# A trunk of attention and HGRN2 heads on one core: a head's output is multiplied and copied out of PSUM before its norm scale is known

## The chip, the core and the metric

One core of a Trainium2 chip runs the whole kernel. TensorE (PE) multiplies matrices and writes only to PSUM; VectorE (DVE) and ScalarE (ACT) read PSUM and SBUF; GpSimd (POOL) works on SBUF; SyncE (SP) issues most of the transfers. Each engine works through its own queue in order, and semaphores tie the queues together. The metric is the time of one execution on the device in microseconds, as a median of runs.

## What is computed

Two layers run over 256 latent tokens and 256 context tokens of 1024 channels. Each layer mixes tokens with three parallel branches (differential attention, a gated MLP over chunks, a bidirectional HGRN2), merges them, and ends with a convolutional FFN. Layer 0 computes context outputs too (512 tokens), layer 1 only the latent ones (256). What the change touches is the end of the first and the third branch, where each head's output is normed over its 128 channels:

```python
def att_out(o):
    return (rmsnorm(o, att_subln_g) * (1 - lam_init)).reshape(o.shape[0], o.shape[1], ATT_VW)

def hg_out(o, g):
    Bo, To = o.shape[0], o.shape[1]
    o = rmsnorm(o.astype(h.dtype), hg_norm_g) * jax.nn.silu(g.reshape(Bo, To, HG_HEADS, HG_DV))
    return o.reshape(Bo, To, HG_VW)
```

## The kernel before

Each of the two layers goes through a stage of heads, a gMLP stage, a merge of the branches, an output product and an FFN. Weights come from HBM as 128x1024 tiles on SP's queue (L110), are cast to a rounded high part on ScalarE (L111) and a low part on VectorE (L112), and every large product is three matmuls into one PSUM bank (L121 to L123).

In the stage of heads the loop runs over eight heads. While the large products of head h+1 are made ("main": gates L371 to L375, softplus and silu L354 to L363, rotary embedding L577 to L585, values L405), two generators work off head h: `hg_head` and `att_head`. `weave` interleaves them: main is cut into steps, and each generator's `yield`s are spread over them. So TensorE's order is written out by the program (its schedule is set to manual), while ScalarE, VectorE and GpSimd get theirs from a planner, which takes what is ready and, of that, what the program traced first. Nothing in this order changes at run time.

There are two pools of four PSUM banks: "pm" for the large products, "ps" for all else. A head's output `o` is a "ps" tile of 128 channels by NQ tokens (512 in layer 0, 256 in layer 1), which lies in one bank until its last reader is done. For the norm, `rms_square` squares it on ScalarE (L316) and splits the square in a high part (ScalarE, L192) and a low part (VectorE, L193, tile "sqs"). In a later step `rms_scale` sums both over the channels with a product by all ones on TensorE (L321), and takes Ln (L327) and Exp (L328) on ScalarE; the result r is the reciprocal root, in tile "sq".

Then r is multiplied with the output: in `hg_head` by L550, which reads `o`, the norm weight "hgn" and r, and by L551, which multiplies with the gate `gg` (half of the tile "qg"); in `att_head` by L644, which reads `o`, the factor `av[:, 1:2]` and r. The result is stored to HBM on SP's queue (L943) and read again in the merge. So `o` holds its bank over the ones product, Ln, Exp, and L550 or L644.

Around this place VectorE also works off the levels of the next HGRN head: differences L441 (followed by an Exp, L442, on ScalarE), products L445, and the masked copies L465 from a "ps" bank; and attention's scores (L602 on TensorE, maxima L605 on VectorE, Exp L608 on ScalarE), turned weights (L619, L621, tile "wt" with two buffers), and value products (L626). GpSimd multiplies in L447, L460, L579 and L585.

Of the kernel before, what the change touches and what calls it, by code (L numbers as in the profile page):

```python
# [13 lines left out]
AF = mybir.ActivationFunctionType  # L14
# [3 lines left out]
P = 128  # L18
# [29 lines left out]
def trunk(ctx: ExitStack, tc: tile.TileContext, A, out):  # L48
    nc = tc.nc
    sub, mul, add, amin, amax = ALU.subtract, ALU.mult, ALU.add, ALU.min, ALU.max  # L50
# [9 lines left out]
    @contextmanager  # L60
    def pool(name, side="left", **tags):
        with tc.tile_pool(name=name, bufs=1, side=side, reuse_waits="tile") as p:
            def get(tag, shape, dt=F32):
                return p.tile(shape, dt, tag=tag, name=tag, bufs=tags[tag])
            yield get
# [10 lines left out]
    def PS(shape):  # L76
        return psm.tile(shape, F32, tag="ps", name="ps")
# [22 lines left out]
    def pk(l, n):  # L100
        a, b = PK[n]
        return pack[l][:, a:b]
# [88 lines left out]
    def split(t, src):  # L191
        nc.scalar.copy(out=t[:, 0, :], in_=src)  # L192
        nc.vector.tensor_tensor(out=t[:, 1, :], in0=src, in1=t[:, 0, :].bitcast(F32), op=sub)  # L193
        return t
# [119 lines left out]
    def rms_square(get, o, n):  # L314
        sq = get("sq", [P, 512])
        nc.scalar.activation(out=sq[:, :n], in_=o, func=AF.Square)  # L316
        return sq, split(get("sqs", [P, 2, n], F32R), sq[:, :n])
# [5 lines left out]
    def rms_scale(sq, n):  # L323
        sq, parts = sq
        ms = PS([P, 512])
        column_sums(ms[:, :n], parts)
        nc.scalar.activation(out=sq[:, :n], in_=ms[:, :n], func=AF.Ln, scale=1.0 / P, bias=epsb)  # L327
        nc.scalar.activation(out=sq[:, :n], in_=sq[:, :n], func=AF.Exp, scale=-0.5)  # L328
        return sq
# [78 lines left out]
    def hg_head(get, l, h, z, k, q, gg, v, put, lbv, C0, NQ):  # L408
# [3 lines left out]
        if l > 0:  # L412
            s = get("E", [P, 2, NT])
            nc.scalar.activation(out=s, in_=z, func=AF.Exp)
            for d in range(2):
                nc.vector.tensor_scalar(out=s[:, d, :], in0=s[:, d, :], scalar1=lbv[:, 1, d, h:h + 1], scalar2=2.0 ** -60,
                                        op0=mul, op1=amax)
                nc.scalar.activation(out=s[:, d, :], in_=s[:, d, :], func=AF.Ln, bias=lbv[:, 0, d, h:h + 1])
                nc.vector.scalar_tensor_tensor(out=z[:, d, :], in0=z[:, d, :], scalar=lbv[:, 2, d, h:h + 1], in1=s[:, d, :],
                                               op0=add, op1=amin)  # L420
# [118 lines left out]
        o = PS([P, NQ])  # L539
        for s in range(NS):  # L540
# [3 lines left out]
            if s == 0:  # L544
                for d in range(2):
                    nc.tensor.matmul(o[:, c], lhsT=st[:, d, :], rhs=V[:, d, 0:T], start=False, stop=(d == 1))  # L546
        sq = rms_square(get, o, NQ)
        yield
        r = rms_scale(sq, NQ)
        nc.vector.scalar_tensor_tensor(out=r[:, :NQ], in0=o, scalar=pk(l, "hgn"), in1=r[:, :NQ], op0=mul, op1=mul)  # L550
        nc.vector.tensor_tensor(out=r[:, :NQ], in0=r[:, :NQ], in1=gg, op=mul)  # L551
        put(r[:, :NQ])

# [34 lines left out]
    def att_head(get, l, qk, v, put, av, NQ):  # L588
        sc = 64 ** -0.5
        o = None  # L590
# [39 lines left out]
        for i in range(n + 2):  # L630
# [3 lines left out]
            if 2 <= i:  # L634
                if o is None:
                    o = PS([P, NQ])
                values(i - 2, *ws.pop(i - 2))
            if 1 <= i <= n:
                ws[i - 1] = turn(*ps.pop(i - 1))
                yield  # L640
        sq = rms_square(get, o, NQ)
        yield
        r = rms_scale(sq, NQ)
        nc.vector.scalar_tensor_tensor(out=r[:, :NQ], in0=o, scalar=av[:, 1:2], in1=r[:, :NQ], op0=mul, op1=mul)  # L644
        put(r[:, :NQ])
        yield

# [193 lines left out]
    with pool("x0", side="right", x=4, n=4, h=4, wa=5, wb=5, scr=1, cr=1, wj=1) as get, \  # L841
# [19 lines left out]
        av = cp.tile([P, 2, 8], F32, tag="av00", name="av")  # L861
# [31 lines left out]
        for t0 in (0, 2):  # L893
            r = []
# [41 lines left out]
    for l in range(DEPTH):  # L936
        ns = 4 if l == 0 else 2
        NQ = ns * P
# [28 lines left out]
        with pool("heads", lk=2, qg=1, qk=1, v=3, w=2, sq=2, sqs=2 if l else 1, wt=2, sc=1, E=6 if l else 4, K=2, p=2) as get, ExitStack() as even, \  # L967
# [22 lines left out]
            for h in range(HEADS):  # L990
                j = slice((h % 2) * P, (h % 2 + 1) * P)
                m = [hg_head(get, l, h, d["ls"], d["k"], d["qg"][:, 0, :], d["qg"][:, 1, :], d["vh"][:, :, j], putter(1, h),
                             lbv, (reset, masks), NQ),
                     att_head(get, l, d["qk"], d["va"][:, :, j], putter(0, h), attv[l], NQ)]
                if h + 1 < HEADS:
                    main, n = project(h + 1, d), units(h + 1)
                else:
                    even.close()
                    getv = rvt.enter_context(pool("vt", side="right", vt=ns))
                    vt = [getv("vt", [P, D]) for _ in range(ns)]  # L1000
                    pus = []
                    main, n = tail_proj(l, Xh, vt, ns, NQ, pus), 8 * ns // 2 + ns
                weave(main, n, m, (13, 2 * ns + 3), 0.92 if h + 1 < HEADS else (0.7, 0.85)[l])
# [4 lines left out]
        with pool("off", off=1) as off, pool("yT", yT=4) as get, ExitStack() as ygpool:  # L1008
            off("off", [P, (64, 48)[l]])
            yT = [get("yT", [P, 2, NQ]) for _ in range(4)]  # L1010
            get = ygpool.enter_context(pool("yg", ws=2, yg=4))
# [200 lines left out]
```

## Time and profile before

| | us |
|---|---|
| median of 3 runs | 2232.55 |
| lowest, highest | 2230.82, 2233.64 |
| profiled execution, its own time | 2240.42 |
| its span, first to last instruction | 2238.6 |
| mean granted TensorE clock in it | 0.981 of full speed |

The profile is that of one execution. Busy times are per engine; the share of a stretch is what matters, since the stages have different limits. The two stages of heads lie at about 100 to 640 us (layer 0) and 1440 to 1850 us (layer 1). A group's mean mixes shapes unless the view keeps them apart, and a wait is put down to the instruction that came last.

### The profile page before, as it was taken

To read this page: it belongs to the slowest core of one execution; us is meant where nothing else is said; L and a number is where in the kernel's file an instruction comes from. 1 tells how busy PE (TensorE), PEld (TensorE's weight loads), DVE (VectorE), ACT (ScalarE), POOL (GpSimd) and SP (SyncE) were. 2 spreads that over 40 slices of the span, in tenths; PEclk is the share of its full clock that TensorE was granted. 3 is DMA by queue.
4 is the path that set the end of the run, shared out by engine and by line. 5 is a ranking of instruction groups with operands and counts; after the bars stand their busy time and mean duration, and the time that the engine had idled before them with its cause. 6 is when DMAs were issued, how large, how long until landed. Compare 5 with 4: busy or idle time off the path is not lost. (4 is left out here: it accounts for less than half of the span.)

```text
span 2238.6 us, 32836 instructions
## 1 busy us (share of the span) xinstructions
PE 2136.9 (95%) x12448; PEld 1860.9 (83%) x12448; DVE 1713.4 (77%) x2869; ACT 1155.8 (52%) x1920; POOL 315.7 (14%) x272
## 2 busy tenths in 40 slices
PE   8999999999999998989999998999999989997998
PEld 7888788887888886878887877988888879997997
DVE  6799888989767884358776766898899976567786
ACT  3766665656543223245342334666666655455664
POOL 3332132322200000011000002222221210001000
PEclk9999999999999999999999999999999999998999
DMA  7212212212255754344555653322222336654554
GB/s 283 94 67 73 70 66 76 73 65 66 62 174 193 235 161 112 94 159 136 166 187 182 198 148 105 104 91 90 81 90 86 97 99 218 195 183 142 186 194 138
DMA packets 93488, 293.21 MB, mean 131 GB/s; under 512 B 16017, under 2 KB 20753, under 8 KB 93073
## 3 DMA queue, kind: packets, MB, share of 16 engines
q1 hardware_dynamic: 93042, 290.59, 40.1%
q8 instruction: 98, 1.61, 0.3%
q14 instruction: 60, 0.49, 0.1%
q10 hardware_dynamic: 288, 0.52, 0.1%
HBM read 282.66 MB, written 8.41 MB: 130 GB/s over the span
## 5 line engine op out<-in xcount | busy, mean ns | idle before, releaser
L121 PE MATMUL pm<-X,wh 128*128 128x512 f32 (+1 forms) x2032 | 716.1, 352 | 11.0 <-DVE X L255 6.5
L122 PE MATMUL pm<-X,wh 128*128 128x512 f32 (+1 forms) x2032 | 699.0, 344 | 0.0
L123 PE MATMUL pm<-X,wl 128*128 128x512 f32 (+1 forms) x2032 | 698.8, 344 | 0.0
L112 DVE TENSOR_TENSOR wl<-wr,wh 128x1024 fp32r<-128x1024 f32 (+1 forms) x402 | 496.8, 1242 | 203.5 <-ACT wh L111 198.9
L111 ACT CAST wh<-wr 128x1024 fp32r<-128x1024 f32 x408 | 422.0, 1039 | 310.7 <-PE pm L122 172.2
L121 PEld LDWEIGHTS pm<-X,wh 128*128 128x128 f32 x2032 | 386.8, 190 | 61.2 <-DVE X L255 7.9
L123 PEld LDWEIGHTS pm<-X,wl 128*128 128x128 f32 x2032 | 387.1, 190 | 47.3
L122 PEld LDWEIGHTS pm<-X,wh 128*128 128x128 f32 x2032 | 386.5, 190 | 42.1
L225 DVE SCALAR_TENSOR_TENSOR wj<-wa,scr 128x1024 f32<-128x1024 f32 x128 | 156.4, 1222 | 63.4 <-DMA wa<-in_ada_row 60.4
L447 POOL TENSOR_TENSOR K<-qg,E 128x512 f32<-128x512 f32 (+1 forms) x96 | 132.3, 1380 | 461.9 <-PE ps L507 304.3
L121 PE MATMUL pm<-wl,X 128*128 128x256 f32 (+1 forms) x608 | 188.0, 309 | 0.0
L122 PE MATMUL pm<-wh,X 128*128 128x256 f32 (+1 forms) x608 | 183.7, 302 | 0.0
L123 PE MATMUL pm<-wh,X 128*128 128x256 f32 (+1 forms) x608 | 183.7, 302 | 0.0
L202 POOL TENSOR_TENSOR s<-s,mhalf 128x1 f32<-128x1 f32 x26 | 14.3, 550 | 1078.4 <-DVE s L199 1052.7
L121 PE MATMUL pm<-ys,wh 128*128 128x512 f32 (+1 forms) x384 | 129.9, 338 | 10.6 <-ACT wh L111 7.4
L441 DVE TENSOR_TENSOR E<-lk 128x512 f32<-128x512 f32 (+1 forms) x192 | 124.4, 681 | 9.5 <-PE ps L546 8.1
L123 PE MATMUL pm<-ys,wl 128*128 128x512 f32 (+1 forms) x384 | 129.5, 337 | 0.0
L122 PE MATMUL pm<-ys,wh 128*128 128x512 f32 (+1 forms) x384 | 129.5, 337 | 0.0
L121 PEld LDWEIGHTS pm<-wl,X 128*128 128x128 f32 x608 | 117.7, 194 | 6.5 <-issue 2.2
L122 PEld LDWEIGHTS pm<-wh,X 128*128 128x128 f32 x608 | 117.8, 194 | 4.0
L123 PEld LDWEIGHTS pm<-wh,X 128*128 128x128 f32 x608 | 117.4, 193 | 4.2
L442 ACT ACTIVATE E<-E 128x1024 f32<-128x1024 f32 (+1 forms) x96 | 80.9, 846 | 59.9 <-DVE E L441 58.9
(250 smaller groups left out, 3541.3 us busy)
## 6 DMA issues: line engine op xcount, KB each, us to landing
wr<-in_w_up SPq DMA_DIRECT2D x88, 512.0 KB, 4.4
wa<-in_ada_row SPq DMA_DIRECT2D x80, 512.0 KB, 4.1
wr<-in_w_gate SPq DMA_DIRECT2D x48, 512.0 KB, 4.0
wr<-in_w_dn SPq DMA_DIRECT2D x40, 512.0 KB, 4.1
wr<-in_w_hqg SPq DMA_DIRECT2D x32, 512.0 KB, 3.6
wr<-in_w_hff SPq DMA_DIRECT2D x32, 512.0 KB, 3.6
wr<-in_w_aqk SPq DMA_DIRECT2D x32, 512.0 KB, 3.6
wr<-in_w_hi SPq DMA_DIRECT2D x16, 512.0 KB, 4.0
```

The source lines that it names most:

```text
L111: nc.scalar.copy(out=hi, in_=raw)
L112: eng.tensor_tensor(out=lo, in0=raw, in1=hi.bitcast(F32), op=sub)
L121: nc.tensor.matmul(ps, lhsT=lh, rhs=rl, start=first, stop=False)
L122: nc.tensor.matmul(ps, lhsT=lh, rhs=rh, start=False, stop=False)
L123: nc.tensor.matmul(ps, lhsT=ll, rhs=rh, start=False, stop=last)
L202: nc.gpsimd.tensor_tensor(out=r, in0=r, in1=mhalf, op=ALU.pow)
L225: nc.vector.scalar_tensor_tensor(out=junk, in0=raw, scalar=1.0, in1=scr[:, v, :], op0=mul, op1=mul, accum_out=mod[l][:, m, v:v + 1])
L441: nc.vector.tensor_tensor(out=dst, in0=ref if first else src, in1=src if first else ref, op=sub)
L442: nc.scalar.activation(out=E, in_=E, func=AF.Exp)
L447: nc.gpsimd.tensor_tensor(out=mkap(KQ[:], dims, NQ), in0=mkap(q, dims), in1=mkap(E[:], [[2 * b, np_], [b - NQ, 2], [1, b]], NQ), op=mul)
```

## The change

Both normalisations read `o` ahead of the `yield` that follows the square, and no more behind it.

In `hg_head` the product of `o` with the norm weight and the gate is made first, in place of the gate's tile, on VectorE; behind the Exp one product with r is left. The number of VectorE instructions and their sizes stay.

In `att_head` ScalarE copies `o` times the factor to a tile `u`, taken from the tag "wt" of the turned weights; behind the Exp VectorE multiplies r with `u`, both in SBUF, in place of the product that read `o` from PSUM. Each head has one ScalarE instruction more, 16 in all.

```diff
@@ hg_head
         sq = rms_square(get, o, NQ)
+        nc.vector.scalar_tensor_tensor(out=gg, in0=o, scalar=pk(l, "hgn"), in1=gg, op0=mul, op1=mul)
         yield
         r = rms_scale(sq, NQ)
-        nc.vector.scalar_tensor_tensor(out=r[:, :NQ], in0=o, scalar=pk(l, "hgn"), in1=r[:, :NQ], op0=mul, op1=mul)
         nc.vector.tensor_tensor(out=r[:, :NQ], in0=r[:, :NQ], in1=gg, op=mul)
         put(r[:, :NQ])
@@ att_head
         sq = rms_square(get, o, NQ)
+        u = get("wt", [P, NQ])
+        nc.scalar.activation(out=u, in_=o, func=AF.Copy, scale=av[:, 1:2])
         yield
         r = rms_scale(sq, NQ)
-        nc.vector.scalar_tensor_tensor(out=r[:, :NQ], in0=o, scalar=av[:, 1:2], in1=r[:, :NQ], op0=mul, op1=mul)
+        nc.vector.tensor_tensor(out=r[:, :NQ], in0=r[:, :NQ], in1=u, op=mul)
         put(r[:, :NQ])
         yield
```

## Rows read from the trace of the kernel before

**Rows 1.** The page's first part: busy us of an engine, share of span, instructions.

```profile
PE 2136.9 (95%) x12448; PEld 1860.9 (83%) x12448; DVE 1713.4 (77%) x2869; ACT 1155.8 (52%) x1920; POOL 315.7 (14%) x272
```

**Rows 2.** Stretches of heads: stretch, length, busy us by engine, granted clock, DMA.

```profile
core 0: us, PE busy (x) PEld busy (x) DVE busy (x) ACT busy (x) POOL busy (x), PEclk, DMA share, GB/s
100.00:640.00 540.00, 521.65 (x3010) 443.95 (x3009) 453.92 (x781) 323.32 (x566) 144.61 (x89) 0.99 0.21 71
1440.00:1850.00 410.00, 388.93 (x2551) 343.68 (x2550) 360.87 (x718) 262.64 (x502) 86.10 (x91) 0.98 0.28 91
```

**Rows 3.** Waits of TensorE: who waited for whom: us in total, times, longest.

```profile
PE ps L321 <- DVE sqs L193: 17.0, 13, 2.7
...
PE ps L626 <- DVE sc L465: 4.6, 3, 1.5
```

**Rows 4.** Views of lines L644, L550, L551: ns min/median/max, first and last start, forms.

```profile
L644 DVE SCALAR_TENSOR_TENSOR sq<-ps,attv,sq x16: 469/610/751, 148.4 to 1836.7; 128x512 f32<-128x512 f32 x8, 128x256 f32<-128x256 f32 x8
...
who waited for it (us, times):
busy tenths in 40 slices 0000000000000000000000000000000000000000
...
L550 DVE SCALAR_TENSOR_TENSOR sq<-ps,pack,sq x16: 470/610/751, 161.3 to 1849.1; 128x512 f32<-128x512 f32 x8, 128x256 f32<-128x256 f32 x8
...
L551 DVE TENSOR_TENSOR sq<-sq,qg x16: 405/553/1225, 162.6 to 1849.6; 128x512 f32<-128x512 f32 x8, 128x256 f32<-128x256 f32 x8
```

**Rows 5.** Waits of ScalarE, in the same columns.

```profile
ACT X L251 <- DVE h L250: 23.0, 23, 3.6
```

**Rows 6.** ScalarE's groups by shape: count, busy us, mean ns, idle before.

```profile
L272 ACT ACTIVATE n<-x,s 128x512 f32<-128x512 f32 x10 | 7.2, 723 | 4.3 <-POOL s L202 4.3
...
L621 ACT COPY wt<-ps 128x512 f32<-128x512 f32 x16 | 9.3, 583 | 0.4 <-PE ps L619 0.4
...
L621 ACT COPY wt<-ps 128x256 f32<-128x256 f32 x16 | 5.8, 362 | 3.7 <-PE ps L619 3.3
```

**Rows 7.** Timeline, an even head of layer 1: start, length, instruction, [idle before <-releaser].

```profile
1584.12 0.38 ACT L316 ACTIVATE sq<-ps 128x256 f32<-128x256 f32 x1 [1.36 <-PE ps L546]
...
1585.72 2.50 DVE L441 TENSOR_TENSOR E<-lk 128x256 f32<-128x256 f32 x4
...
1588.48 0.94 DVE L193 TENSOR_TENSOR sqs<-sq,sqs 128x256 fp32r<-128x256 f32 x1
...
1594.04 0.47 DVE L550 SCALAR_TENSOR_TENSOR sq<-ps,pack,sq 128x256 f32<-128x256 f32 x1
1594.43 0.47 DVE L458 TENSOR_TENSOR E<-E,lk 128x256 f32<-128x256 f32 x1
```

**Rows 8.** An odd head of layer 1: VectorE's timeline, then the chain that ended last.

```profile
1547.13 0.17 DVE L473 COPY s<-E 128x4 f32<-128x4 f32 x1 [1.89 <-ACT E L470]
...
1551.89 0.40 DVE sq L550
```

**Rows 9.** VectorE's timeline in an even head of layer 0.

```profile
289.64 2.39 DVE L441 TENSOR_TENSOR E<-lk 128x512 f32<-128x512 f32 x2
291.95 0.68 DVE L193 TENSOR_TENSOR sqs<-sq,sqs 128x512 fp32r<-128x512 f32 x1
```

**Rows 10.** The 20 us around one wait of L321, columns as in rows 2.

```profile
1580.00:1600.00 20.00, 17.31 (x97) 15.43 (x96) 18.20 (x36) 9.98 (x21) 6.83 (x7) 0.83 0.19 66
```

**Rows 11.** Timeline behind attention's square in layer 1: ScalarE's, then VectorE's.

```profile
1577.81 0.42 ACT L362 ACTIVATE t<-t 128x256 f32<-128x256 f32 x1
...
1578.36 0.41 DVE L363 TENSOR_TENSOR qg<-t,pm 128x256 f32<-128x256 f32 x1
```

**Rows 12.** VectorE's timeline: one HGRN gate product of layer 0.

```profile
162.61 0.69 DVE L551 TENSOR_TENSOR sq<-sq,qg 128x512 f32<-128x512 f32 x1
```

## The prediction

> **What bounds the kernel now.** I read the page's busy table first. TensorE is marked busy for 2136.9 of 2238.6 us, VectorE for 1713.4, ScalarE for 1155.8 [rows 1]. A busy TensorE is not a TensorE at its peak, so the second view is the table by stretch, cut to the two stretches in which heads run, the only ones that the change touches. VectorE is busy there 453.9 of 540 us in layer 0 (84%) and 360.9 of 410 us in layer 1 (88%), ScalarE 60% and 64%, and TensorE is marked idle for 18.4 and 21.1 us [rows 2]. So in these stretches VectorE's queue is nearly as full as TensorE's, and a small step matters only where one of the two waits for the other.
>
> The third view is the list of waits. TensorE waits most for the split of the squared head output (L193), ahead of the all-ones product L321: 17.0 us in 13 waits, up to 2.7 us each [rows 3]. By place these are the attention splits of the four even heads of layer 0, the HGRN splits of two of those heads, and the HGRN splits of all heads of layer 1 but the last (seven). The nearest thing to a wait for a PSUM bank is the value product L626 behind the masked copy L465, 4.6 us in 3 waits [rows 3]: there a bank is given free by L465, not by a normalisation. The fourth view is that of one line. At L644, the read that now closes attention's bank, the list of those who waited for it is empty, and L550's answer has no entry there either [rows 4]. **Nobody waits for the bank that the change sets free sooner.**
>
> **The change part by part.** The sum is made against the profiled execution: span 2238.6 us, 2240.42 us in all, which is 7.87 us above the median of 2232.55 us. I carry differences over to the median unchanged.
>
> *Bank released earlier.* The read L550 or L644 no longer stands behind the ones product, Ln and Exp. Worth at most the 4.6 us of bank waits if they had been for that bank; L465 is named instead, so I take 0.
>
> *VectorE in attention.* L644 (0.47 to 0.75 us, median 0.61) becomes a plain product of two SBUF tiles, whose like is L551 (0.41 to 1.23 us, median 0.55) [rows 4]. Sixteen heads by 0.06 us: -0.9 us of VectorE work at the medians. I take -0.9. The other bound is that every one is as slow as the slowest L551 (1.23): 16 x (1.23 - 0.61) = +9.9 us, further than I believe (see the rivals).
>
> *ScalarE copy in attention.* It adds 16 operations with a per-channel factor. Their shape without a factor is L621: 583 ns for 512 columns, 362 for 256; the same function with a factor, SBUF to SBUF, is L272: 723 ns for 512 [rows 6]. So 0.58 to 0.72 us in layer 0 and, with the same 0.14 us added, 0.36 to 0.50 us in layer 1 (an estimate from these rows): 7.5 to 9.8 us of ScalarE work. I take the upper value, since L272 has the factor. What hides it is ScalarE's idle 36 to 40% [rows 2]; where the queue is dense it is not hidden. It can run as soon as the square L316 is done and, since the cast must wait for the square's result, it will probably slip between the two, in a place where other work stands today. Queued behind it are the cast, the next head's softplus steps and the weight casts L111. In layer 1 the dense place shows: ScalarE's L362 ends at 1578.23 and VectorE's L363, which needs it, starts at 1578.36 [rows 11]. A delay of 0.4 us arrives at VectorE there, in up to seven heads: 0 to +2.8 us. In layer 0 I see no such place: where TensorE waits for an attention split there, the cast is long done and VectorE is late. I take +1.3. The copy also holds a "wt" buffer; the next head turns its weights into such a buffer only behind its first two score steps, so 0.
>
> *HGRN's product moved up.* The number of VectorE instructions stays, and so do their sizes. L550 reads one PSUM and one SBUF tile before and after. What changes is its place. Two engines that only read one bank are still put in order: ScalarE's L251 waits 23.0 us in 23 waits for VectorE's L250, and both only read the same bank [rows 5]. So the product comes behind the square L316, not beside it, and is ready while ScalarE still casts. Ahead of the split, then, VectorE has one more instruction to choose from, 0.39 us at 256 columns (1594.04 to 1594.43, [rows 7]) and, estimated by the same overlap from 0.75, 0.67 us at 512. Three cases, by head:
> - Even heads of layer 1 (four): after the square at 1584.12 come four L441 and others, then the split at 1588.48 for which TensorE stands still [rows 7]. If the product is only added to that queue, the split is 0.39 later: 4 x 0.39 = +1.6. If it takes the place of one L441, which then goes behind the split, 0 or a gain of that L441's time, 0.4 to 0.6: 4 x -0.6 = -2.4.
> - Odd heads of layer 1 with a next head (three): VectorE idles for 1.89 us ahead of L473 just when the product becomes ready, while the product's present place at 1551.89 is on the chain that ended last [rows 8]: 3 x -0.39 = -1.2. The bound on the other side is 0 (0.39 added ahead of the split, the same taken away behind it).
> - Even heads of layer 0 (four): two slow L441 (2.39 us) stand before the split at 291.95 [rows 9]. Added to the queue: two to four x 0.67 = +1.3 to +2.7. Filling the time of the cast so that the split is next: up to one L441 (1.2 us) less in each of two heads, -2.4. The other heads have no TensorE wait at the split, hence 0.
> Together -6.0 to +4.3; I take 0, since the instruction is ready in a stretch that other ready work fills today, and the split has to wait for its cast either way. Behind L551 only the store L943 waits, and the store's data is read again in a later stage: 0.
>
> *TensorE's clock.* In the 20 us around the 2.7 us wait at 1589 the granted clock was 0.83 of full speed [rows 10], that is, in part at 1.2 instead of 2.4 GHz: 0.17 x 20 = 3.4 us of TensorE's speed in all. Stalls before L321 that grow or shrink may bring such a fall or take one away: -3.4 to +3.4 us; I take 0.
>
> **Sum:** 0 - 0.9 + 1.3 + 0 + 0 = +0.4 us, so 2240.8 us in the manner of the profiled execution, and 2233.0 us as a median.
>
> **The rivals.**
> *Slower: the product stands in front of the split.* If VectorE's fixed order is square, product, L441 as before, split, the ones product waits longer in each head in which it waits today. Price: +1.6 + 2.7 (both from above), the ScalarE copy at its bound +2.8, and one more fall of the clock, +3.4, less 0.9: +9.6, or 2242 us. It decides from the point at which the product adds more than some 4.5 us. For it: TensorE waits for the split already [rows 3], and VectorE's queue is 84 to 88% full. Against it: the waiting time of the cast gives room.
> *Faster: the product fills a gap and the splits come forward.* -2.4 - 1.2 - 2.4 from above, -0.9, and one fall of the clock less, -3.4: -10.3, or 2222 us; with half of it 2227. For it: the idle 1.89 us and the chain through L550 [rows 8]. Against it: VectorE's total stays, so what comes forward pushes an L441 back, and that one is on the path too.
> *Slower: the SBUF port.* L551 took 1.23 us at its slowest and 0.69 in another head at the same 512 columns, while L550, with one operand in PSUM, never took over 0.75 [rows 4, 12]. The attention product loses its PSUM operand by this change, so it can be slowed in the same way whenever GpSimd works; GpSimd is busy for 144.6 of 540 and 86.1 of 410 us [rows 2]. At that share 16 x 0.24 x 0.54 = +2.1 us, 2235 us, still no change; at the bound +9.9 us from above, 2242 us. The Trainium skill says it as a rule (page "SBUF — State Buffer", section "Who interferes with whom"): a VectorE instruction with two SBUF inputs contends with a GpSimd instruction that reads SBUF, one with a single SBUF input does not. The rows named agree with that so far as they go.
> *The change does not do what it says:* the bank is free sooner but TensorE never wanted it. That is my forecast, not an exception to it.
>
> **How the numbers follow.** A measurement of this kernel can tell about 0.2%, 4.5 us, from no change. Forecast (all parts within their bounds, cancelling): 0.48, 2228 to 2237 us. Splits come forward: 0.25, 2222 to 2228. Product in front of the split, with a fuller ScalarE: 0.21, 2237 to 2242. Port at its bound: 0.06, 2237 to 2242. So faster 0.25, same 0.48, slower 0.27. The range leaves out about a tenth at either end: 2223 to 2242 us, which covers the two rivals' half prices and nearly their full ones. The predicted time is the forecast's, 2233.0 us.
>
> **What would show it.** In the profile after: no TensorE wait that named a bank of a head output, since none does now; L465 still in front of L626. The copy's row at 0.65 to 0.75 us (512) and 0.45 to 0.55 (256). VectorE's sum in the two stretches lower by about 1 us, ScalarE's higher by 8 to 10. The wait L321 behind the split at 17 us, give or take 4: clearly above, the first rival; clearly below, the second. The attention product's slowest row at 0.7 us or at 1.2. I would be wrong if the order of VectorE or ScalarE changes far from the heads' ends, since a new order there could move more than any term above, or if the copy had to reload ScalarE's tables.

## The result, and the profile after

The changed kernel takes 2252.69 us (median of 4 runs, 2245.02 to 2254.16) against 2233.1 us for the kernel before, run beside it (median of 4): a ratio of 1.0083, 95% interval 1.0058 to 1.0107. It is slower by 0.8%, where no change was forecast, and above the range of 2223 to 2242 us. The profiled execution is the fastest of the four, 2245.02 us with a span of 2243.2.

First the page's busy times and the two stretches of heads, in the columns of [rows 1] and [rows 2]:

```profile
PE 2131.9 (95%) x12448; PEld 1856.0 (83%) x12448; DVE 1717.5 (77%) x2869; ACT 1163.2 (52%) x1936; POOL 302.0 (13%) x272
...
100.00:640.00 540.00, 510.66 (x2933) 435.26 (x2933) 450.69 (x776) 319.59 (x565) 129.46 (x89) 0.97 0.20 66
...
1440.00:1850.00 410.00, 388.47 (x2557) 342.41 (x2556) 370.51 (x732) 267.60 (x513) 90.80 (x95) 0.99 0.28 90
```

VectorE's sum is 4 us higher with the same 2869 instructions, ScalarE's 7.4 us with 16 more. In layer 0 TensorE gets through 77 matmuls fewer in the same 540 us, at a granted clock of 0.97 instead of 0.99. The heads of layer 0 are where the time goes. Since TensorE's order is written out, the n-th matmul is the same in both kernels, and their start times can be compared one by one: by 587 us the changed kernel is 17.5 us late, and nearly all of that arises at four places (5.2, 2.9, 5.9 and 5.7 us; some 2 us are won back between them). Behind the heads of layer 0 this one execution wins back 13 us more, so that it ends only 4.6 us after the profiled execution of the kernel before; a second profile (after_again, below) is 18.5 us late at the same matmul and still 15.7 us late at 2200 us.

TensorE's waits in the whole execution, columns as in [rows 3]:

```profile
PE ps L321 <- DVE sqs L193: 20.8, 11, 4.0
...
PE ps L546 <- ACT w L536: 9.2, 5, 2.3
...
PE ps L619 <- DVE sc L465: 5.8, 1, 5.8
PE ps L626 <- DVE sc L465: 4.2, 3, 1.4
```

The wait of L321 behind the split grew only from 17.0 to 20.8 us, but it moved. Cut to 100 to 640 us it was 6.6 us in 6 waits and is now 19.7 in 8:

```profile
PE ps L321 <- DVE sqs L193: 19.7, 8, 4.0
```

From 1440 to 1850 us it fell from 10.3 to 1.0, and there the waits of L546 and L619 came in its place (layer 1 comes out even, see layer1_only). In layer 0 the waits that grew most are those at the HGRN's ones product in the four even heads: 0.4, 1.1, 0.0 and 0.0 us before, 2.5, 2.5, 4.1 and 4.1 after (the time beyond the usual step from one matmul to the next), and 4.1 in all four in a second profile of the same kernel, whose row for the same stretch is:

```profile
PE ps L321 <- DVE sqs L193: 22.1, 8, 4.0
```

No wait names a head output's bank, before or after. The changed lines themselves show what they cost (columns as in [rows 4], then the groups of layer 0 with count, busy us and mean ns as in [rows 6]):

```profile
L646 DVE TENSOR_TENSOR sq<-sq,wt x16: 410/616/1793, 150.4 to 1846.2; 128x512 f32<-128x512 f32 x8, 128x256 f32<-128x256 f32 x8
...
L643 ACT ACTIVATE wt<-ps,attv x16: 465/578/702, 142.6 to 1840.7; 128x512 f32<-128x512 f32 x8, 128x256 f32<-128x256 f32 x8
...
L646 DVE TENSOR_TENSOR sq<-sq,wt 128x512 f32<-128x512 f32 x8 | 8.8, 1096 | 2.7 <-ACT sq L328 2.7
L548 DVE SCALAR_TENSOR_TENSOR qg<-ps,pack,qg 128x512 f32<-128x512 f32 x8 | 6.0, 744 | 5.4 <-ACT sq L316 5.4
```

L646 is attention's product (L644 before), L643 the copy, L548 the moved HGRN product (L550 before). The copy is as forecast. The attention product, which should have become a little cheaper, went from 742 to 1096 ns on average in layer 0.

**One of the four places, read closely.** The stretch runs from attention's ones product to the HGRN's, in the third even head. Timeline of the kernel before (VectorE, then one line of GpSimd), in the columns of [rows 7]:

```profile
419.40 1.10 DVE L441 TENSOR_TENSOR E<-lk 128x512 f32<-128x512 f32 x1
420.42 0.74 DVE L644 SCALAR_TENSOR_TENSOR sq<-ps,attv,sq 128x512 f32<-128x512 f32 x1
...
423.10 0.68 DVE L441 TENSOR_TENSOR E<-lk 128x512 f32<-128x512 f32 x1
423.70 1.21 DVE L112 TENSOR_TENSOR wl<-wr,wh 128x1024 fp32r<-128x1024 f32 x1
424.84 0.82 DVE L458 TENSOR_TENSOR E<-E,lk 128x512 f32<-128x512 f32 x1
425.59 1.27 DVE L441 TENSOR_TENSOR E<-lk 128x512 f32<-128x512 f32 x2
426.79 0.67 DVE L193 TENSOR_TENSOR sqs<-sq,sqs 128x512 fp32r<-128x512 f32 x1
...
422.34 6.34 POOL L585 TENSOR_TENSOR qk<-t,qk 128x256 fp32r<-128x256 f32 x1 [1.24 <-ACT qk L584]
```

The same place after (VectorE, GpSimd, ScalarE, TensorE):

```profile
424.41 0.68 DVE L441 TENSOR_TENSOR E<-lk 128x512 f32<-128x512 f32 x1
425.69 1.09 DVE L445 TENSOR_TENSOR K<-lk,E 128x512 f32<-128x512 f32 x1
427.41 0.42 DVE L583 TENSOR_TENSOR t<-t,sh 128x256 f32<-128x256 f32 x1 [0.64 <-POOL sh L579]
...
429.10 1.78 DVE L646 TENSOR_TENSOR sq<-sq,wt 128x512 f32<-128x512 f32 x1
...
431.14 1.03 DVE L458 TENSOR_TENSOR E<-E,lk 128x512 f32<-128x512 f32 x1
432.09 0.68 DVE L441 TENSOR_TENSOR E<-lk 128x512 f32<-128x512 f32 x1
432.69 2.31 DVE L112 TENSOR_TENSOR wl<-wr,wh 128x1024 fp32r<-128x1024 f32 x1
434.93 1.28 DVE L441 TENSOR_TENSOR E<-lk 128x512 f32<-128x512 f32 x2
436.13 0.74 DVE L548 SCALAR_TENSOR_TENSOR qg<-ps,pack,qg 128x512 f32<-128x512 f32 x1
436.79 0.67 DVE L441 TENSOR_TENSOR E<-lk 128x512 f32<-128x512 f32 x1
437.39 0.68 DVE L193 TENSOR_TENSOR sqs<-sq,sqs 128x512 fp32r<-128x512 f32 x1
...
428.52 1.81 POOL L429 TENSOR_TENSOR w<-w,qg 128x512 f32<-128x512 f32 x1 [1.14 <-DVE w L428]
430.29 1.18 POOL L585 TENSOR_TENSOR qk<-t,qk 128x256 fp32r<-128x256 f32 x1
432.25 1.67 POOL L460 TENSOR_TENSOR E<-E,qg 128x512 f32<-128x512 f32 x1 [0.78 <-DVE E L458]
...
435.70 1.06 ACT L442 ACTIVATE E<-E 128x1024 f32<-128x1024 f32 x1 [3.53 <-DVE E L441]
436.66 0.60 ACT L192 CAST sqs<-sq 128x512 fp32r<-128x512 f32 x1
...
438.21 1.19 PE L321 MATMUL ps<-sqs,onesr 128*128 128x512 f32 x2 [3.91 <-DVE sqs L193]
```

Three things are to be seen. (1) The moved product L548 stands in front of the split, 0.74 us. (2) Three VectorE instructions with both operands in SBUF take longer, each beside an SBUF product of GpSimd that is under way when they start (L429, which the list of GpSimd's lines above leaves out, L585 and L460): L646 1.78 instead of 0.74 for L644, L112 2.31 instead of 1.21, L458 1.03 instead of 0.82. L646 starts inside GpSimd's L429 (428.52 to 430.33) and ends 0.55 us behind it; L112 starts inside L460 (to 433.92) and ends 1.08 behind it: each looks stopped until GpSimd is done, and then takes about its usual time. Before, it was the other way round: GpSimd's L585 took 6.34 us, beside a dense row of VectorE work that ran at its usual pace, and 1.18 after. (3) ScalarE's planned order has the next head's Exp L442 ahead of the cast; it waits 3.53 us for VectorE's L441, and the cast behind it.

The same place as a table by windows (columns as in [rows 2]), of before from one ones product to the next and the 7 us behind it:

```profile
418.20:427.80 9.60, 9.60 (x47) 8.19 (x48) 9.60 (x17) 7.07 (x12) 8.37 (x3) 1.00 0.22 82
...
427.80:434.80 7.00, 6.52 (x53) 6.22 (x53) 5.37 (x9) 4.81 (x8) 5.80 (x5) 1.00 0.24 78
```

and of after:

```profile
424.50:438.20 13.70, 9.76 (x46) 7.99 (x47) 13.06 (x20) 7.53 (x12) 7.49 (x5) 0.94 0.16 57
...
438.20:445.20 7.00, 6.99 (x37) 6.81 (x38) 3.75 (x7) 3.58 (x7) 1.96 (x2) 0.63 0.33 116
```

Before, TensorE and VectorE are both busy for all 9.60 us: **VectorE has no gap at all there**, and TensorE waits for nothing by luck of a tie: the split ends at 427.46 and the ones product starts at 427.76. What is added to VectorE beyond that 0.3 us is added to TensorE's path. So it is in three of the four even heads; in the second VectorE idles for 1.27 us, until a weight cast of ScalarE is done, and TensorE waits already. After, the stretch is 4.1 us longer. On VectorE, up to the end of the split, 2.35 us of that are the three slowed instructions, 0.64 the gap ahead of L583, which is a wait for GpSimd too, 0.66 the product (436.13 to 436.79), and 0.60 one L441 more than before that now stands ahead of the split (five in place of four). The L445 at 425.69 takes 1.09 us, as the L441 at 419.40 did, each beside GpSimd's L447. Then TensorE, having stood still, is granted 0.63 of full speed for the next 7 us instead of 1.00, that is, in part 1.2 instead of 2.4 GHz, and by the start times of the same matmuls another 1.6 us go.

On point 2 the Trainium skill (page "SBUF — State Buffer", section "Who interferes with whom") says that VectorE instructions with two SBUF inputs and GpSimd's reads share a port, and that the order of issue decides which of them blocks. Both directions are in the rows above. The order of issue fits L646 and L112, which start behind GpSimd's product, but not the kernel before: there L585 starts at 422.34, and L112, L458, the L441 beside them and the split start behind it and run at their usual time.

### The profile page after: what moved, and what is told of

It reads as the page before. It is cut to its first block, busy times and chain, and to the rows that moved or that the text cites. A ratio compares the mean times of both kernels' runs of the same rounds, so it can differ in the third digit from the quotient of the medians.

```text
span 2243.2 us, 32845 instructions
## 1 busy us (share of the span) xinstructions
PE 2131.9 (95%) x12448; PEld 1856.0 (83%) x12448; DVE 1717.5 (77%) x2869; ACT 1163.2 (52%) x1936; POOL 302.0 (13%) x272
## 5 line engine op out<-in xcount | busy, mean ns | idle before, releaser
L121 PE MATMUL pm<-X,wh 128*128 128x512 f32 (+1 forms) x2032 | 713.7, 351 | 11.2 <-DVE X L255 6.9
L112 DVE TENSOR_TENSOR wl<-wr,wh 128x1024 fp32r<-128x1024 f32 (+1 forms) x402 | 501.7, 1254 | 198.7 <-ACT wh L111 192.8
L447 POOL TENSOR_TENSOR K<-qg,E 128x512 f32<-128x512 f32 (+1 forms) x96 | 127.3, 1328 | 492.6 <-PE ps L507 304.9
L441 DVE TENSOR_TENSOR E<-lk 128x512 f32<-128x512 f32 (+1 forms) x192 | 121.2, 666 | 11.1 <-PE ps L546 9.7
L442 ACT ACTIVATE E<-E 128x1024 f32<-128x1024 f32 (+1 forms) x96 | 80.9, 844 | 60.8 <-DVE E L441 59.8
```

Of the source, the lines that this page charges most:

```text
L112: eng.tensor_tensor(out=lo, in0=raw, in1=hi.bitcast(F32), op=sub)
L121: nc.tensor.matmul(ps, lhsT=lh, rhs=rl, start=first, stop=False)
L441: nc.vector.tensor_tensor(out=dst, in0=ref if first else src, in1=src if first else ref, op=sub)
L442: nc.scalar.activation(out=E, in_=E, func=AF.Exp)
L447: nc.gpsimd.tensor_tensor(out=mkap(KQ[:], dims, NQ), in0=mkap(q, dims), in1=mkap(E[:], [[2 * b, np_], [b - NQ, 2], [1, b]], NQ), op=mul)
```

## The experiments

The measure that ties most of them together is the length of that stretch, summed over the four even heads of layer 0, from the start times of L321 in the trace. The letters of the theories in the expectations hold for one text each; theory A is every time the lateness at the ones product in these heads, with its cause as I saw it then. Kernels in which TensorE's order is untouched (in the last four, which come further down, single instructions are held back):

| kernel | stretches, us | sum | ratio to before, 95% interval |
|---|---|---|---|
| layer1_only | 9.9, 9.6, 9.6, 9.6 | 38.6 | 1.0000, 0.9983 to 1.0017 |
| before | 9.9, 12.2, 9.6, 9.6 | 41.3 | 1 |
| all_but_even_heads | 10.0, 12.8, 9.9, 9.9 | 42.6 | 0.9998, 0.9975 to 1.0021 |
| hgrn_both_att_layer1 | 10.0, 12.2, 10.0, 12.0 | 44.2 | 0.9995, 0.9978 to 1.0013 |
| hgrn_only | 12.2, 12.0, 10.0, 10.0 | 44.2 | 0.9989, 0.9973 to 1.0006 |
| dead_copy | 12.9, 10.0, 12.2, 10.0 | 45.1 | 1.0007, 0.9989 to 1.0024 |
| without_two_gpsimd_products | 11.8, 11.8, 11.8, 11.8 | 47.3 | 1.0017, 1.0002 to 1.0033 |
| att_only | 13.6, 13.0, 11.2, 11.2 | 49.0 | 1.0025, 1.0009 to 1.0042 |
| copy_on_vector | 12.5, 12.5, 12.5, 12.5 | 50.1 | 1.0063, 1.0039 to 1.0087 |
| r_in_psum | 13.1, 13.1, 13.1, 13.1 | 52.4 | 1.0045, 1.0027 to 1.0062 |
| after | 13.7, 13.7, 13.7, 13.7 | 54.7 | 1.0083, 1.0058 to 1.0107 |
| after_again | 13.7, 13.7, 13.7, 13.7 | 54.7 | 1.0090, 1.0062 to 1.0118 |
| layer0_only | 13.7, 13.7, 13.7, 13.7 | 54.7 | 1.0075, 1.0051 to 1.0098 |
| after_cast_first | 9.6, 9.6, 9.6, 9.6 | 38.3 | 1.0036, 1.0020 to 1.0053 |
| exps_and_product_behind | 9.6, 9.6, 9.6, 9.6 | 38.3 | 1.0067, 1.0043 to 1.0090 |
| differences_behind_too | 9.5, 9.5, 9.5, 9.5 | 38.0 | 1.0068, 1.0045 to 1.0091 |
| before_differences_behind | 9.5, 9.5, 9.5, 9.5 | 38.0 | 1.0037, 1.0020 to 1.0053 |

But for the last four, time follows the stretches, though not to the microsecond: the stretches are those of one execution and single executions of one kernel differ by 5 to 10 us either way, and the first 3 to 4 us of growth cost nothing that can be measured. The 12.2 us in the second head of the kernel before belong to that one execution: layer1_only has the same order there and 9.6 us.

**Which part?** The changed kernel was measured again, and each part alone (hgrn_only keeps L644 and has no copy; att_only keeps L550 behind the Exp).

```diff
# hgrn_only, against the kernel before
+        nc.vector.scalar_tensor_tensor(out=gg, in0=o, scalar=pk(l, "hgn"), in1=gg, op0=mul, op1=mul)
-        nc.vector.scalar_tensor_tensor(out=r[:, :NQ], in0=o, scalar=pk(l, "hgn"), in1=r[:, :NQ], op0=mul, op1=mul)
# att_only, against the kernel before
+        nc.scalar.activation(out=u, in_=o, func=AF.Copy, scale=av[:, 1:2])
-        nc.vector.scalar_tensor_tensor(out=r[:, :NQ], in0=o, scalar=av[:, 1:2], in1=r[:, :NQ], op0=mul, op1=mul)
+        nc.vector.tensor_tensor(out=r[:, :NQ], in0=r[:, :NQ], in1=u, op=mul)
```

> The changed kernel once more, for a second profile. Both theories: 1.006 to 1.011 of the kernel before, and the even heads of layer 0 some 15 to 18 us longer than before in total, since the order of every queue is the same as in the first profile. What is open is whether the 5 us that the first profile gained behind the heads of layer 1 (products that the change does not touch) come again; if they do not, they belong to that one execution, and the usual 2253 us is this profile without them.

> Only the HGRN part of the change: norm weight and gate multiplied ahead of the scale, attention as before. Theory A (the loss is ScalarE's order: in the even heads of layer 0 the cast of the square stands behind a level's Exp that waits for VectorE, and it is the added attention copy that brought this order): here the cast stands right behind the square in layer 0 as before, and in the even heads of layer 1 too, where an Exp stood between before, so 4 to 10 us faster, 2223 to 2229 us, with the waits for L321 down from 17 to under 10 us. Theory B (the product itself, 0.4 to 0.7 us ahead of the split on VectorE, makes TensorE wait): 5 to 17 us slower, waits for L321 over 20 us.

> Only the attention part: ScalarE copies the output times the factor, HGRN as before. Theory A: the new order on ScalarE comes with the copy; in three of four even heads of layer 0 no Exp stands between square and cast, but VectorE has its weight split L112 and three level differences ahead of the split, so layer 0 is 2 to 10 us longer and layer 1 a few us shorter: 2230 to 2242 us. Theory B: without the HGRN product there is nothing more ahead of the split: 2231 to 2235 us, waits for L321 at 17 us.

The second profile and time of the changed kernel came out as the first (1.0090). Alone, the HGRN part costs nothing that can be measured (0.9989, 2231.84 us, between the ranges of both theories) and the attention part 0.25% (2237.15 us, in theory A's range); together they cost 0.8 to 0.9%. The stretches add up in the main (2.9 and 7.7 us of growth, 13.4 together), the times do not.

**Which layer, which heads?** The parts were switched by layer and by head.

```diff
# layer1_only: if l == 1    layer0_only: if l == 0    all_but_even_heads: if l == 1 or h % 2 == 1
# hgrn_both_att_layer1: HGRN part always, attention part if l == 1
```

> The whole change in layer 1 alone, layer 0 as before. Theory A: the loss is in the even heads of layer 0 (some 18 us in the trace of the changed kernel), while layer 1 gains about 7 us up to its last head and gives 3 back there: 2225 to 2231 us. If the loss were spread over both layers: 2238 to 2246 us.

> HGRN part in both layers, attention part in layer 1 alone. Theory A: no copy in layer 0, so the cast stays right behind its square there, and layer 1 as in the changed kernel: 2225 to 2231 us, the same as with the change in layer 1 alone. Theory B (the HGRN product costs in layer 0 by itself): 3 to 10 us more than with the change in layer 1 alone.

> The whole change in layer 0 alone. Theory A (all of the loss arises in the even heads of layer 0): 2247 to 2256 us, ratio to before 1.006 to 1.010. Rival C (the loss needs both layers or arises behind the heads): under 2243 us.

> The whole change in layer 1 and in the odd heads of layer 0; the four even heads of layer 0 as before. Theory A (the loss sits in these four heads): 2229 to 2238 us, ratio 0.998 to 1.002, and the waits of L321 in those heads at most 1 us each as before. Rival D (the odd heads of layer 0 carry part of it): 2240 us or more.

The first came to 2234.57 us, the second to 2235.11, the third to 2252.22, the fourth to 2233.15: all of the loss that can be measured is in layer 0, and leaving its four even heads as they were takes it away. The gain of some 7 us that I had expected of layer 1 is not there. TensorE's first wait in layer0_only, which has the new waits of layer 0 and the old ones of layer 1:

```profile
PE ps L321 <- DVE sqs L193: 30.6, 15, 4.0
```

and in layer1_only, which has neither, with its two new ones (L622 is L619 there):

```profile
PE ps L321 <- DVE sqs L193: 6.0, 8, 1.8
...
PE ps L546 <- ACT w L536: 9.3, 5, 2.3
PE ps L622 <- DVE sc L465: 6.3, 1, 6.3
```

Layer 1 thus trades one wait for two others and comes out at 1.0000.

**The copy's own work?** dead_copy is the kernel before with the copy added, its result read by nothing. copy_on_vector is the whole change with the copy on VectorE.

```diff
# dead_copy
+        nc.scalar.activation(out=u, in_=o, func=AF.Copy, scale=av[:, 1:2])
# copy_on_vector
-        nc.scalar.activation(out=u, in_=o, func=AF.Copy, scale=av[:, 1:2])
+        nc.vector.tensor_scalar(out=u, in0=o, scalar1=av[:, 1:2], scalar2=None, op0=mul)
```

> The kernel before plus the attention copy on ScalarE, whose result nothing reads: both normalisations read their bank where they did. Theory A (the loss of the attention part is the added ScalarE instruction and the order that it brings to both queues: in the even heads of layer 0 the weight split L112 and three level differences now stand on VectorE between square and split): as the attention part alone or a little slower, 2235 to 2242 us, waits for L321 at 18 to 22 us. Theory C (it is the changed product behind the Exp, or the bank set free sooner): as before, 2231 to 2235 us.

> The whole change, but the attention copy runs on VectorE in place of ScalarE: 16 instructions of 0.4 to 0.7 us, some 8 us of VectorE work more and none on ScalarE. Theory A: ScalarE's order in layer 0 stays as before (only one other instruction between square and cast, and that not a level's Exp in the first head), L112 stands ahead of the square again, so in spite of the work added 2230 to 2239 us, well below the changed kernel. Theory C (reading the bank early is what costs): 2248 to 2256 us.

Sixteen ScalarE instructions as such cost nothing that can be measured (1.0007): 2236.46 us lies in theory A's range, but the kernel before took 2234.89 beside it. The interval still overlaps that of att_only. With the copy on VectorE the kernel takes 2246.54 us, between the ranges of both theories: it loses 0.63% with an attention product that is never slowed (684 ns in layer 0):

```profile
L646 DVE TENSOR_TENSOR sq<-sq,wt 128x512 f32<-128x512 f32 x8 | 5.5, 684 | 2.8 <-ACT sq L328 2.8
...
427.43 1.91 DVE L455 TENSOR_TENSOR E<-lk 128x512 f32<-128x512 f32 x1
432.98 1.11 DVE L193 TENSOR_TENSOR sqs<-sq,sqs 128x512 fp32r<-128x512 f32 x1
...
426.98 1.66 POOL L429 TENSOR_TENSOR w<-w,qg 128x512 f32<-128x512 f32 x1 [0.62 <-DVE w L428]
431.90 1.65 POOL L460 TENSOR_TENSOR E<-E,qg 128x512 f32<-128x512 f32 x1 [3.26 <-DVE E L458]
```

The copy itself is not in the stretch: in the third even head it starts at 419.18 us, ahead of attention's ones product at 421.63. The stretch is 12.5 us all the same, in the main because GpSimd's products now hold up other instructions, two of them in the rows behind the first: L455, 1.91 us instead of 0.83, and the split itself, 1.11 instead of 0.68. L112 is at its usual 1.21. So what matters is that VectorE's time in this stretch grows, whichever instruction is held up.

**Is it the wait at L321, or what the queues hold?** In after_cast_first the level Exps L442 and L457 are issued behind the last cast; in exps_and_product_behind only in the even heads of layer 0, and the HGRN product behind the split; in differences_behind_too the differences L441 as well; before_differences_behind does that to the kernel before. Names in the lines below are shortened.

```diff
# after_cast_first
+            with tc.issue_after(last_cast):
                 nc.scalar.activation(out=E, in_=E, func=AF.Exp)
# exps_and_product_behind, in even heads of layer 0 (differences_behind_too: the L441 too)
+            with tc.issue_after(cast):
                 nc.scalar.activation(out=E, in_=E, func=AF.Exp)
+        with tc.issue_after(split):
             nc.vector.scalar_tensor_tensor(out=gg, in0=o, scalar=pk(l, "hgn"), in1=gg, op0=mul, op1=mul)
```

> The whole change, and in addition the Exps of levels and pairs (L442, L457) are made to be issued on ScalarE behind the last cast of a squared head output. No work is added or removed. Theory A: the four waits of 2.5 to 4.1 us for L321 in the even heads of layer 0 fall to about 1 us or less, 10 to 15 us less than the changed kernel, 2236 to 2243 us. Theory B: the product still stands ahead of the split: 2248 to 2254 us, as the changed kernel.

> The whole change; in the even heads of layer 0 the next head's Exps (L442, L457) are issued behind the cast and the HGRN product behind the split. All work stays. Theory A, in the form that these two places make the loss: the four waits of 2.5 to 4.1 us at L321 and the falls of the clock behind them go, 2229 to 2238 us. Rival B (the order elsewhere, which the same planning changes, makes it): 2243 to 2256 us.

> As exps_and_product_behind, and the next head's differences L441 behind the split too. Theory A: 2226 to 2236 us, the waits of L321 in layer 0 all but gone, unless the differences, pushed back, come late for the next head's products (then 2236 to 2245, with L546 or L626 in TensorE's list).

> The kernel before with the next head's differences and Exps behind the split in the even heads of layer 0. There the HGRN splits make TensorE wait only 0.0 to 1.1 us, so theory A expects little: 2226 to 2236 us. If it is slower than 2238, the order by itself costs and differences_behind_too is to be compared with it, not with the kernel before.

after_cast_first came to 1.0036 (2242.11 us, in theory A's range), exps_and_product_behind to 1.0067, differences_behind_too to 1.0068, before_differences_behind to 1.0037. The waits at the HGRN's ones product in layer 0 are gone in all four (each of the stretches is 9.5 to 9.6 us long), and yet some two fifths of the loss are still there in the first, and four fifths in the two that pin the even heads of layer 0, that is, hold single steps back there alone. TensorE's longest list entry in exps_and_product_behind (L628 is the transposes of attention's weights, L619 before):

```profile
PE ps L628 <- DVE s L615: 12.2, 6, 3.3
```

The wait went 35 us down the road, to the next head's attention: 9.9 of these 12.2 us are three waits in layer 0, where there was none. Pinned in the same way, the kernel before shows such waits too (11.7 us in 7). Here my expectations of 2229 to 2238 and 2226 to 2236 us failed, and so did that of 2226 to 2236 for the pinned kernel before (2241.44): the Exp and the product in front of the split are how the lateness shows, not all of its cause. And the kernel before loses 0.4% by the same pinning alone; next to it the change still costs some 0.3% (1.0068 against 1.0037), with stretches of the same length.

The other way is to issue the ones product later: the scale step of each head goes to the start of the next head (after_late, before_late, hgrn_late).

```diff
-        r = rms_scale(sq, NQ)   # and the products, and the store
+        fins.append(finish)     # the same steps, run at the first step of the next head
```

> The changed kernel; of each head the scale step behind the square (ones product, Ln, Exp, products, store) is issued later, at the start of the next head, and attention's last empty step stands ahead of its scale step. All work stays. Theory A (the loss is TensorE standing at the ones product L321 in the even heads of layer 0, with the fall of the clock behind it): the waits of the ones product for the split, 20.8 us in the changed kernel, go to under 6, the time goes from 2252 to 2225 to 2238 us. Rival B (the loss is work that VectorE and ScalarE have in their queues, wherever TensorE stands): 2246 to 2256, and the waits turn up in front of other TensorE instructions.

> The same later scale step in the kernel before. Theory A: the 17.0 us of waits ahead of the ones product go to under 6, 2216 to 2230 us, unless the head's output, which now holds its bank until then, makes score or value products wait for a bank (then 2230 to 2250, with a wait for L550 or L644 in TensorE's list). Rival B: 2230 to 2240.

> The HGRN part of the change alone, with the later scale step. Theory A: as the kernel before with it, 2215 to 2230 us. Rival B: 2229 to 2237. If theory A holds and the two parts together still cost, this is 10 us or more under the whole change with the later step.

They came to 1.0038 (1.0024 to 1.0053), 1.0050 (1.0033 to 1.0067) and 1.0054 (1.0035 to 1.0074). None is in the range of a theory A (2243.75, 2245.72 and 2246.85 us; before_late has no wait for a head output's bank either), so as an improvement it failed: attention's scores (L613, L602 before) wait longer for GpSimd's rotary product (4.0 us in 4 waits before), as in after_late:

```profile
PE ps L613 <- POOL qk L596: 13.7, 5, 3.7
...
PE ps L321 <- DVE sqs L193: 6.1, 2, 4.5
```

Compared with each other they still say something: with the ones product late, the change costs nothing that can be measured (1.0038 against 1.0050 without it), while in the old place it costs 0.8%.

**The port.** r_in_psum lets attention's Exp write r to PSUM, so that its product has one operand there. without_two_gpsimd_products leaves out GpSimd's products L429 and L460, and with them two factors of the result. In both the planned order of VectorE and ScalarE around the split is that of the changed kernel.

```diff
# r_in_psum
-        nc.scalar.activation(out=sq[:, :n], in_=sq[:, :n], func=AF.Exp, scale=-0.5)
+        nc.scalar.activation(out=ms[:, :n], in_=sq[:, :n], func=AF.Exp, scale=-0.5)
# without_two_gpsimd_products
-        nc.gpsimd.tensor_tensor(out=kd, in0=kd, in1=q, op=mul)
-            nc.gpsimd.tensor_tensor(out=W, in0=W, in1=q, op=mul)
```

> The whole change, but attention's Exp writes r to PSUM, in place of the ones product's result, so that the attention product has one PSUM and one SBUF operand. Port theory: its slowest falls from 1.79 to under 0.8 us, the stalls of 4.1 us at the HGRN's ones product in the even heads of layer 0 shrink by about 1 us each, 2243 to 2250 us against 2252. Rival (order alone): the stalls and the time stay, 2249 to 2256 us.

> The whole change without GpSimd's products L429 and L460 (two factors are left out of what is computed). Port theory: the attention product at 0.7 us, the weight's low part at 1.2 us, VectorE's work between the two ones products 11 to 12 us instead of 14.0, the stalls at the HGRN's ones product 1 to 2 us instead of 2.5 to 4.1, and 2235 to 2245 us. Rival (order alone): stalls of 3.5 us or more and 2248 to 2256 us.

VectorE's timeline in the third even head of r_in_psum (L647 is the attention product, L442 the differences):

```profile
429.78 0.69 DVE L647 TENSOR_TENSOR sq<-ps,wt 128x512 f32<-128x512 f32 x1
...
431.65 1.22 DVE L442 TENSOR_TENSOR E<-lk 128x512 f32<-128x512 f32 x1
432.80 2.29 DVE L112 TENSOR_TENSOR wl<-wr,wh 128x1024 fp32r<-128x1024 f32 x1
```

The attention product is back at 0.69 us, but L442 now meets GpSimd (1.22 instead of 0.68) and L112 still does: 0.6 us a head are won, not 1.1. The time, 1.0045 or 2245.33 us, lies in the range expected of the port, but is lower by more than these 0.6 us explain; the intervals of 1.0045 and 1.0083 leave room for less. Without the two GpSimd products:

```profile
424.58 1.23 DVE L644 TENSOR_TENSOR sq<-sq,wt 128x512 f32<-128x512 f32 x1
...
427.41 1.22 DVE L112 TENSOR_TENSOR wl<-wr,wh 128x1024 fp32r<-128x1024 f32 x1
```

L112 and L458 are back at their usual times, the attention product (L644 here) is at 1.23, still beside the rotary product. The stretch is 11.8 us instead of 13.7, TensorE waits 2.3 us instead of 4.1, and the kernel is at 1.0017, inside the 2235 to 2245 us expected. So with the same order and the same product in front of the split, taking GpSimd's two instructions away removes about four fifths of the loss. Part of that may be other work that the missing products made easier; the same was not tried on the kernel before. But the 1.9 us a head are accounted for by the slowed instructions alone: 1.09 (L112), 0.55 (attention product), 0.21 (L458).

**What is settled and what is not.** Settled: the loss arises in the four even heads of layer 0, where TensorE waits for VectorE's split and its clock falls behind the wait. But for one head of one execution VectorE has no gap there, so its time is TensorE's. It grew by VectorE instructions that GpSimd held up and by a wait for GpSimd, 3.0 us of some 4.3 in the head shown, more than by the moved product (0.66) and the L441 that came forward (0.60). The product's share is less plain than that: in att_only's first even head VectorE's order is that of the changed kernel without the product, and the stretch is 13.6 us all the same, with the split 0.49 us late for its cast.

Which engine is held up does not hang on the planned order alone. In hgrn_only all four even heads have one order: in the last two GpSimd's L585 takes 5.14 us, VectorE runs at its usual pace, and the stretch is 10.0 us; in the second L585 takes 1.43, VectorE's L441 (1.23 and 1.76 us) and the split (1.10) are held up, and the stretch is 12.0. Nor does a held-up engine always cost: before, and in two heads of dead_copy, it was GpSimd (6.34 and 5.97 us), and TensorE waited 0.4 us at most. The changed kernel has a slowed L112 and the product in all four heads, in both profiles.

That this is why two parts which cost little alone cost 0.8% together is argued from these rows; no run set both in an otherwise unchanged order. Open as well: what decides which engine goes first; why holding back single steps costs as much elsewhere, beyond that each moved the wait to another instruction; and where the 0.3% between the two pinned kernels lies, with stretches of 9.5 us in both. No version was clearly faster than the kernel before.

## Why the prediction was wrong, point by point

- *Bank released earlier, 0:* right. Nobody waits for a head output's bank, before or after.
- *Copy, +1.3 us:* the size was right (0.70 us at the longest and 0.47 at the shortest, within 0.58 to 0.72 for 512 columns and 0.36 to 0.50 for 256; ScalarE's sum is up by 7.4 us against 7.5 to 9.8). The delay in layer 1, bound +2.8, is not to be seen: layer1_only is at 1.0000, with an interval of 3.8 us either way that does not rule it out.
- *VectorE in attention, -0.9 us:* wrong in sign. In layer 0 the product went from 742 to 1096 ns, +2.8 us over eight heads. The bound of +9.9 us held, but the value was taken from the median of L551, which runs at another moment. With one operand in PSUM the product is back at 684 ns (r_in_psum).
- *HGRN's product moved, 0:* right for the product alone (hgrn_only at 0.9989), and its length was right (0.66 us of the queue against 0.67). **The step that failed is the overlap, on the way from the parts to the sum.** The terms for VectorE's work ahead of the split in the even heads of layer 0 (0 here, -0.9 above) took the instructions around it in today's order and at today's length, and went by "a small step matters only where one of the two waits for the other". But where both engines are busy without a gap, an added instruction is an added wait: the two even heads whose wait is 0.0 us have a split that ends 0.3 us ahead of its ones product, which is no wait, but no slack either. What the runs showed in its place: with both edits in, the stretch grew from 9.6 to 13.7 us, 0.66 of it by the product and 3.0 by GpSimd holding VectorE up; with the falls of the clock that made the kernel 17.5 us late by the end of layer 0's heads.
- *Clock, 0 with 3.4 either way:* the mechanism was right, the size was for one fall where there are four: some 1.6 us each.
- *The rival "product in front of the split"* named the place, the wait ahead of the split, and had 0.21. By itself it does not hold: hgrn_only has the product there and costs nothing. Its 2242 us were 10 too low, since the price left out that instructions around the product can be slowed, and took one fall of the clock. The sign I had named for it, a wait at L321 clearly above 17 us, give or take 4, did not show in the sum over both layers (20.8 us), since layer 1's fall hid layer 0's rise.
- *The rival "SBUF port"* had the rule and the right row [rows 4, 12], but was priced by GpSimd's mean share of the time and as plain VectorE work, +2.1 us. The hits fall together in the one place where VectorE is full (on the attention product in three of the four heads in the first profile, on L112, which the diff does not touch, in all four), and there each microsecond is TensorE's, with the clock on top. The two slower rivals were also kept apart, with a chance for each; they came together.
- *The planned order* was named as what would make the forecast wrong and was given neither a price nor a chance.

## What to carry to other kernels

Before a moved or added instruction is costed at nothing, look at the window between the two products that wait for its engine, not at the stage: where both engines are busy for all of it, a wait of 0.0 us is a tie and not slack. An instruction that trades its PSUM operand for a second SBUF one can be held up by GpSimd, so look for GpSimd's work at that very moment and price up to the whole GpSimd instruction. Two edits that cost nothing and 0.25% alone can cost 0.8% together where a planner orders the queues; measure them together, and switch them by stage to find the place.

## What was not expected of the hardware

That the same pair of engines loses time in either direction: GpSimd's L585 took 6.34 us beside VectorE's row of SBUF products, and VectorE's L112 went from 1.21 to 2.31 us and the attention product from 0.68 to 1.78 beside GpSimd's. The first cost this kernel nothing that its waits show, the second is on its path, and the same order of the queues can give either (hgrn_only).
